# Right-side tiles at multiples of 64 bytes, stores and loads moved to ACT's queue at two stage changes, and a new order of a few products

## The chip, the cores and the metric

The kernel runs on one core of a Trainium2 chip. The metric is the device time of one launch in microseconds (us), smaller is better; a time is given as the median of several runs, and one further execution was taken with the hardware profiler.

The engines are named as the profile names them: PE (matrix products; PEld is its loading of weights), DVE, ACT and POOL (elementwise work), and SP, which only starts DMAs here. Each engine works through its own list of instructions in order; an instruction that waits holds all that stand behind it. SP and ACT can both start DMAs.

## What is computed

One decoder block on x (1024 tokens, width 1024, float32), cut to what matters:

```python
xn   = rms_norm(x, norm1_g)
proj = xn @ w_in                                  # q, k, v | q, f, i, g | two gates
o_sb = stick_breaking_attention(q, k, v)          # 8 heads of 64
o_hg = hgrn2_mixer(q_hg, f_hg, i_hg, g_hg)        # 4 heads of 128, a scan over chunks of 64
y_sb, y_hg = o_sb @ w_branch[:512], o_hg @ w_branch[512:]
mixed = sigmoid(gate_sb) * y_sb + sigmoid(gate_hg) * y_hg
h    = x + mixed @ w_out
hn   = rms_norm(h, norm2_g)
out  = h + (silu(hn @ w_gate) * (hn @ w_up)) @ w_down    # hidden width 2816
```

All of it is float32 to float32 accuracy.

## The kernel before

A float32 product is made of three products of halves: `split` (L229 to L239) rounds an operand to a high part (ACT's CAST) and takes the rest as a low part (DVE's subtraction), and PE multiplies high by high, high by low and low by high. The names in the profile end in h and l for the two parts; a group `f<-fh,oh` has its output first, then the moving operand (128x512, the tokens' side) and then the weights. Every large product is 128 partitions by 512 columns.

The stages, in order:

- Stage 1, to about 702 us: the projection, attention and the scan, laid out by a planner of its own (all on L182). The change leaves its order as it is but for one memset on POOL.
- The merge, about 702 to 791.5 us: `oo`, the outputs of the two branches (`oh0` to `oh7`, `ol0` to `ol7`), moves against `w_branch`: 384 products.
- The wo stage, 791.5 to 878.6 us: `mx` (`ah`, `al`) moves against `w_out`: 384 products in 16 groups, one per row block k and half h of the tokens. Behind each group DVE adds x (`xx`, loaded on SP at L856), SP stores the sum to `h_d` in DRAM (L860), ACT squares it and POOL adds the square to `rr` (L870), the sum for the second norm. DVE and ACT then make the operands `fop` (`fh`, `fl`, L846) of the next stage from it, among them the differences `t5`, `t6`, `t7`.
- The gate and up products, 878.6 to 1317.6 us: a fast product after Strassen and Winograd, seven half-size products instead of eight, for gate and for up, for each of NP = 11 slices p of the hidden width (`winograd`, L963; `prod`, L909; every matmul is on L916): 11 x 2 x 7 x 4 blocks x 3 = 1848 matmuls, with `fop` moving. For the first of all, `begin` is `channel_sums`: it turns `rr` into the norm's factor with four matmuls (L929). At the end of each p, SP stores the activations to `act_d`: one tile `c` of 1 MB (L1008) and four tiles `bs` of 256 KB (L1017).
- The down stage, 1317.6 to 1535.6 us: seven products o in the order `DOWN` (1, 2, 6, 7, 4, 5, 3), each of 11 steps p with four banks d and three matmuls: 132 matmuls for each o. For a step SP loads `ra` (from `wd` or `wd_d`) and `rb` (from `act_d`), 256 KB each; ACT and DVE split both. After o = 1, ACT copies the four banks to `acc1` while the banks go on with o = 2. The residual `h_d` is loaded to `hb` in 16 pieces of 256 KB (L1069), all on SP behind o = 1's last loads, and DVE adds banks and `acc1` to it (L1076, L1077) ahead of the stores to `outT` (L1079).

From the merge on the order within an engine is a scheduler's, made from the order of the code and from the buffers that each instruction needs.

Memory: pools on the left side grow upwards, those with `side="right"` downwards from the top. On the right lie `oo`, `fop` and its sources, some constants and masks of stage 1, and `khl`, `qhh`, `qlz` (attention's keys and queries); on the left `xn`, `mx`, all weights' halves, and `ah`, `al`, `bh`, `bl` of the down stage. In the built kernel the tiles on the right start at 32 bytes beyond a multiple of 64 in each partition, those of the left that move against weights at a multiple of 64.

Of the kernel before, what the change touches and what calls it, by code (L numbers as in the profile page):

```python
# [19 lines left out]
P = 128  # L20
# [182 lines left out]
def hybrid_block(ctx: ExitStack, tc, xT, wi, wb, wo, wg, wu, wd, vec, outT):  # L203
# [40 lines left out]

    rst = ExitStack()
# [585 lines left out]
    with tc.tile_pool(name="wot", bufs=4, reuse_waits="tile") as ot_:  # L831
        seq = [0, 4, 1, 5, 2, 6, 3, 7]
        wq = [get_w(wo[seq.pop(0)])]
        for i in range(4):
# [14 lines left out]
            for e in range(2):  # L849
# [4 lines left out]
                for h in range(2):  # L854
# [5 lines left out]
                    nc.sync.dma_start(h_d[k][:, hs(h)], xx)  # L860
# [4 lines left out]
                    if i == 0 and e == 0:  # L865
                        nc.scalar.activation(rr[h], xx, AF.Square)
                    else:
                        sq = tmp("sq")
                        nc.scalar.activation(sq, xx, AF.Square)
                        nc.gpsimd.tensor_tensor(rr[h], rr[h], sq, op=ALU.add)  # L870
# [65 lines left out]
    with ExitStack() as sta:  # L936
# [24 lines left out]
        def winograd(a, c, begin=None):  # L961

            x, y, z = fb(), fb(), fb()  # L963
            p1 = fa.tile([P, HALF], F32, tag="p1", name="p1")
            if begin:
                for ks in ((0, 1, 2), (3,)):
                    for o, bank in ((1, x), (5, z), (6, y)):
                        prod(bank, a[o], fop[o], True, ks)
                begin()
                nc.scalar.copy(p1, x)  # L970
                nc.vector.tensor_tensor(c[:, 1], y, p1, op=ALU.add)
            else:
                prod(x, a[1], fop[1], True)
                nc.scalar.copy(p1, x)
                prod(y, a[6], fop[6], True)
                nc.vector.tensor_tensor(c[:, 1], y, p1, op=ALU.add)
                prod(z, a[5], fop[5], True)
            prod(y, a[7], fop[7], False)
            prod(x, a[2], fop[2], False)
            nc.vector.tensor_tensor(c[:, 3], y, p1, op=ALU.add)  # L980
            nc.vector.tensor_tensor(c[:, 3], z, c[:, 3], op=ALU.add)
            prod(y, a[4], fop[4], False)
            nc.vector.tensor_tensor(c[:, 2], y, p1, op=ALU.add)
            prod(z, a[3], fop[3], False)
            nc.vector.tensor_tensor(c[:, 1], z, c[:, 1], op=ALU.add)
            return x

        ag = left(wpool, wg, 0)
        for p in range(NP):
# [18 lines left out]
            nc.sync.dma_start(act_d[p][:, :4 * HALF], c.rearrange("p b t -> p (b t)"))  # L1008
# [7 lines left out]
            for b, t in ((4, n7), (5, n6), (6, n5), (7, n4)):  # L1016
                nc.sync.dma_start(act_d[p][:, b * HALF:(b + 1) * HALF], t)  # L1017
# [15 lines left out]
          5: [(d + 4, 1) for d in range(4)], 3: [(d, 1) for d in range(4)]}  # L1033
    bank = [None] * 4
    for o in DOWN:
        first = o in (1, 6, 5)
        for p in range(NP):
            early = o == 1 and p < 4
            wp, tags = bp, btags = dB, ("ah", "al")
            btags = ("bh", "bl")  # L1040
            if early:

                rp = wpool if p < 2 else preB
                raw = rp.tile([P, 1024], F32, tag="w", bufs=2, name="w32")
                ra, rb = raw[:, :512], raw[:, 512:]
                if p < 3:
                    wp = bp = rp
                    tags = btags = ("oh", "ol") if p < 2 else ("ds", "ds")
            else:
                ra = dB.tile([P, HALF], F32, tag="ra", name="ra")  # L1050
                rb = dB.tile([P, HALF], F32, tag="rb", name="rb")
            nc.sync.dma_start(ra, LEFT[o](p))
            nc.sync.dma_start(rb, blk(act_d[p], RIGHT[o]))
            hi, lo = split(ra, wp, tags)
            bh, bl = split(rb, bp, btags)
            for d in range(4):
                if first and p == 0:
                    bank[d] = fb()
                ws = slice(d * P, (d + 1) * P)
                nc.tensor.matmul(bank[d], hi[:, ws], bh, start=first and p == 0, stop=False,  # L1060
                                 skip_group_check=True)
                nc.tensor.matmul(bank[d], hi[:, ws], bl, start=False, stop=False,  # L1062
                                 skip_group_check=True)
                nc.tensor.matmul(bank[d], lo[:, ws], bh, start=False, stop=p == NP - 1,  # L1064
                                 skip_group_check=True)
        if o == 1:
            for k, h in ([(d, 0) for d in range(4)] + [(d, 1) for d in range(8)]
                         + [(d, 0) for d in range(4, 8)]):
                nc.sync.dma_start(hb[k][:, hs(h)], h_d[k][:, hs(h)])  # L1069
            for d in range(4):  # L1070
                nc.scalar.copy(acc1[d], bank[d])
            continue
        for d, (k, h) in enumerate(TO[o]):
            t = hb[k][:, hs(h)]
            if o in (6, 7, 4):
                nc.vector.tensor_tensor(t, t, acc1[d], op=ALU.add)  # L1076
            nc.vector.tensor_tensor(t, bank[d], t, op=ALU.add)  # L1077
            if o in (2, 4, 5, 3):
                nc.sync.dma_start(outT[k][:, hs(h)], t)  # L1079
# [48 lines left out]
```

## Time and profile before

| | us |
|---|---|
| median of 3 runs (1540.65 to 1542.45) | 1542.43 |
| the profiled execution | 1541.46 |
| its span | 1539.7 |
| PE busy | 1515.8 (98%) |
| DVE busy | 1184.3 (77%) |
| ACT busy | 800.4 (52%) |
| POOL busy | 178.8 (12%) |

The profile times one execution. The 1.8 us between its time and its span lie around the program. Busy time counts an engine as busy while an instruction runs; matmuls overlap in PE's pipeline, so what one costs is read from the distance between the starts of two. A bracket behind a row, as in [1.08 <-ACT fh L845], gives the idle time of the engine ahead of it and the instruction whose end ended that. [...]

### The profile page before, as it was taken

Reading aid. Unit: us, or ns where it says so; the run is one execution under the profiler, and the core shown is the slowest. Engines: PE = TensorE matmul, PEld = TensorE weight load, DVE = VectorE, ACT = ScalarE, POOL = GpSimd, SP = SyncE. Lnnn points to the kernel's source line nnn. Section 1 sums busy time; section 2 is a strip of 40 time slices with the busy share of each in tenths; the row PEclk is TensorE's granted clock in tenths of the full one; section 3 lists DMA queues with packets and bytes.
Section 4 is the critical chain, followed back from the end, with each engine's and each line's share of the span. In section 5 each row is a group of like instructions: output and inputs, shape, how many; then the busy total and the mean of one; then the engine's idle time right before and its main releaser. Section 6 shows DMA issues by size and latency. Waiting matters only on the chain.

```text
span 1539.7 us, 20478 instructions
## 1 busy us (share of the span) xinstructions
PE 1515.8 (98%) x7213; PEld 1242.1 (81%) x7213; DVE 1184.3 (77%) x2046; ACT 800.4 (52%) x1503; POOL 178.8 (12%) x202
## 2 busy tenths in 40 slices
PE   8999999999999999999999989999999999999999
PEld 6788888888888888888888868778778888778887
DVE  8899679988898768965567798888877777475553
ACT  7866778678768778454333352233333333254442
POOL 4211111111111101114412200000000000000000
PEclk9999999999999999999999999999999999999999
DMA  5111211111111121245334455666633332787672
GB/s 178 41 43 44 76 33 42 59 39 52 50 52 41 59 69 48 71 160 201 125 107 133 139 163 205 217 211 208 213 136 110 105 105 94 270 274 220 193 220 92
DMA packets 78407, 188.53 MB, mean 122 GB/s; under 512 B 9056, under 2 KB 11104, under 8 KB 76896
## 3 DMA queue, kind: packets, MB, share of 16 engines
q1 hardware_dynamic: 73696, 178.83, 35.5%
q10 hardware_dynamic: 4608, 8.39, 1.5%
q8 instruction: 57, 0.93, 0.3%
q14 instruction: 46, 0.38, 0.1%
HBM read 131.61 MB, written 55.57 MB: 122 GB/s over the span
## 4 chain that ended last, share of the span: by engine, by line
PE 73%; DVE 11%; DMA 6%; ACT 4%; issue 4%; POOL 1%; SPq 1%; DVEq 0%; POOLq 0%; ACTq 0%
PE f L916 25%; PE pj L182 23%; PE ms L182 8%; PE f L1062 4%; PE f L1064 4%; PE f L1060 4%; PE z L182 2%; DMA xx<-xT 2%; DVE ol L238 1%; ACT aa L182 1%; DMA rb<-act_d 1%; POOL s L805 1%; DMA s<-sig_d 1%; DVE aa L182 1%; DVE tail L182 1%
## 5 line engine op out<-in xcount | busy, mean ns | idle before, releaser
L182 PE MATMUL pj<-ah,oh 128*128 128x512 f32 x704 | 286.7, 407 | 2.0 <-POOL oh L182 2.0
L182 PE MATMUL pj<-ah,ol 128*128 128x512 f32 x704 | 277.3, 394 | 0.9 <-DVE ol L182 0.9
L182 PE MATMUL pj<-al,oh 128*128 128x512 f32 x704 | 276.0, 392 | 0.0
L916 PE MATMUL f<-fh,oh 128*128 128x512 f32 x616 | 244.0, 396 | 3.4 <-ACT p L970 1.7
L916 PE MATMUL f<-fl,oh 128*128 128x512 f32 x616 | 243.4, 395 | 0.7 <-DVE fl L846 0.7
L916 PE MATMUL f<-fh,ol 128*128 128x512 f32 x616 | 243.2, 395 | 0.6 <-DVE ol L238 0.6
L237 ACT CAST oh<-w 128x512 fp32r<-128x512 f32 x168 | 102.1, 620 | 175.2 <-PE f L916 137.9
L182 PEld LDWEIGHTS pj<-ah,ol 128*128 128x128 f32 x704 | 132.6, 188 | 31.6 <-DVE ol L182 2.1
L182 PEld LDWEIGHTS pj<-ah,oh 128*128 128x128 f32 x704 | 133.1, 189 | 25.3 <-POOL oh L182 2.9
L182 PEld LDWEIGHTS pj<-al,oh 128*128 128x128 f32 x704 | 133.2, 189 | 22.9 <-issue 0.5
L916 PEld LDWEIGHTS f<-fh,oh 128*128 128x128 f32 x616 | 115.4, 187 | 34.3 <-ACT p L970 2.1
L916 PEld LDWEIGHTS f<-fh,ol 128*128 128x128 f32 x616 | 115.4, 187 | 29.1 <-DVE ol L238 1.0
L916 PEld LDWEIGHTS f<-fl,oh 128*128 128x128 f32 x616 | 115.5, 187 | 29.0 <-DVE fl L846 1.0
L238 DVE TENSOR_TENSOR ol<-w,oh 128x512 fp32r<-128x512 f32 x168 | 114.7, 690 | 30.0 <-ACT oh L237 29.8
L1062 PE MATMUL f<-bl,ah 128*128 128x512 f32 x296 | 117.0, 395 | 1.3 <-DVE bl L238 1.3
L1060 PE MATMUL f<-bh,ah 128*128 128x512 f32 x296 | 114.6, 391 | 3.7 <-ACT bh L237 3.7
L182 DVE TENSOR_TENSOR_SCAN aa<-aa,ww 128x128 f32<-128x128 f32 (+3 forms) x96 | 92.3, 975 | 33.4 <-ACT aa L182 23.8
L182 POOL TENSOR_SCALAR oh<-w 128x512 fp32r<-128x512 f32 x84 | 70.9, 844 | 394.0 <-PE pj L182 348.6
L1064 PE MATMUL f<-bh,al 128*128 128x512 f32 x296 | 116.6, 394 | 0.0
L238 DVE TENSOR_TENSOR al<-ra,ah 128x512 fp32r<-128x512 f32 x73 | 50.4, 690 | 72.0 <-ACT ah L237 71.9
L237 ACT CAST ah<-ra 128x512 fp32r<-128x512 f32 x73 | 45.5, 623 | 101.8 <-PE f L1062 93.7
L182 ACT ACTIVATE aa<-aa 128x512 f32<-128x512 f32 (+3 forms) x128 | 69.1, 552 | 4.9 <-DVE aa L182 4.0
(273 smaller groups left out, 2996.7 us busy)
## 6 DMA issues: line engine op xcount, KB each, us to landing
w<-wi SPq DMA_DIRECT2D x42, 512.0 KB, 3.6
rb<-act_d SPq DMA_DIRECT2D x73, 256.0 KB, 4.1
w<-wg SPq DMA_DIRECT2D x22, 512.0 KB, 3.9
w<-wu SPq DMA_DIRECT2D x22, 512.0 KB, 4.1
w<-wd SPq DMA_DIRECT2D x22, 512.0 KB, 6.8
wd_d<-ds SPq DMA_DIRECT2D x44, 256.0 KB, 5.4
act_d<-c SPq DMA_DIRECT2D x11, 1024.0 KB, 3.9
act_d<-bs SPq DMA_DIRECT2D x44, 256.0 KB, 3.5
```

The costliest lines, as they stand in the source:

```text
L182: fn(*[a.real() if isinstance(a, View) else a for a in args], **{k: v.real() if isinstance(v, View) else v for k, v in kw.items()})
L237: pin(nc.scalar.copy(hi, src))
L238: pin(nc.vector.tensor_tensor(lo, src, hi.bitcast(F32), op=ALU.subtract))
L805: nc.gpsimd.tensor_tensor(s[:, hs(h)], s[:, hs(h)], rr1[h], op=ALU.mult)
L916: nc.tensor.matmul(out, a[i][:, ws], bl[k][j], start=start and k == 0 and i + j == 0, stop=k == 3 and i == 1, skip_group_check=True)
L1060: nc.tensor.matmul(bank[d], hi[:, ws], bh, start=first and p == 0, stop=False, skip_group_check=True)
L1062: nc.tensor.matmul(bank[d], hi[:, ws], bl, start=False, stop=False, skip_group_check=True)
L1064: nc.tensor.matmul(bank[d], lo[:, ws], bh, start=False, stop=p == NP - 1, skip_group_check=True)
```

## The change

1. A tile `edge` of 32 bytes per partition is put at the top of the right side, so that all tiles of the right side lie 32 bytes lower, at multiples of 64. POOL sets it to zero once.
2. In the wo stage, the 16 stores to `h_d` go from SP's queue to ACT's.
3. There, the 14 adds to `rr` go from POOL to DVE.
4. In the first gate product (p = 0) the order is new. Before: products 1, 5, 6 over the blocks 0 to 2, then block 3 of each, then `begin`, then ACT's copy of bank x to `p1`. Now: product 1 whole, the copy, product 5 whole, product 6 over blocks 0 to 2, product 2 (into bank x), block 3 of product 6, then `begin`. Product 2 stood behind product 7 before.
5. The five stores to `act_d` of the last p go to ACT's queue.
6. The 16 loads of `hb` go to ACT's queue, two in each of the steps p = 3 to 10 of o = 1.
7. In the last of the down products (o = 3) the last three steps run bank by bank: bank 0 takes its nine matmuls, then its add and its store follow, then bank 1. The loop body is cut into `operands`, `step` and `finish` for that.

The diff, with the parts that only regroup the down loop left out:

```diff
+    edge = ctx.enter_context(tc.tile_pool(name="edge", bufs=1, side="right"))
+    nc.gpsimd.memset(edge.tile([P, 8], F32, name="edge"), 0.0)
     rst = ExitStack()
...
-                    nc.sync.dma_start(h_d[k][:, hs(h)], xx)
+                    nc.scalar.dma_start(h_d[k][:, hs(h)], xx)
...
-                        nc.gpsimd.tensor_tensor(rr[h], rr[h], sq, op=ALU.add)
+                        nc.vector.tensor_tensor(rr[h], rr[h], sq, op=ALU.add)
...
             if begin:
-                for ks in ((0, 1, 2), (3,)):
-                    for o, bank in ((1, x), (5, z), (6, y)):
-                        prod(bank, a[o], fop[o], True, ks)
+                prod(x, a[1], fop[1], True)
+                nc.scalar.copy(p1, x)
+                prod(z, a[5], fop[5], True)
+                prod(y, a[6], fop[6], True, range(3))
+                prod(x, a[2], fop[2], False)
+                prod(y, a[6], fop[6], True, (3,))
                 begin()
-                nc.scalar.copy(p1, x)
                 nc.vector.tensor_tensor(c[:, 1], y, p1, op=ALU.add)
...
             prod(y, a[7], fop[7], False)
-            prod(x, a[2], fop[2], False)
+            if not begin:
+                prod(x, a[2], fop[2], False)
...
-            nc.sync.dma_start(act_d[p][:, :4 * HALF], c.rearrange("p b t -> p (b t)"))
+            store = nc.scalar.dma_start if p == NP - 1 else nc.sync.dma_start
+            store(act_d[p][:, :4 * HALF], c.rearrange("p b t -> p (b t)"))
...
-                nc.sync.dma_start(act_d[p][:, b * HALF:(b + 1) * HALF], t)
+                store(act_d[p][:, b * HALF:(b + 1) * HALF], t)
...
+    HB = ([(d, 0) for d in range(4)] + [(d, 1) for d in range(8)] + [(d, 0) for d in range(4, 8)])
+    LAST = 3
...
+        final = o == DOWN[-1]
+        for p in range(NP - LAST if final else NP):
+            ops = operands(o, p)
+            if o == 1 and p >= 3:
+                for k, h in HB[2 * p - 6:2 * p - 4]:
+                    nc.scalar.dma_start(hb[k][:, hs(h)], h_d[k][:, hs(h)])
             for d in range(4):
                 if first and p == 0:
                     bank[d] = fb()
...
+                step(d, p, ops, first and p == 0)
         if o == 1:
-            for k, h in ([(d, 0) for d in range(4)] + [(d, 1) for d in range(8)]
-                         + [(d, 0) for d in range(4, 8)]):
-                nc.sync.dma_start(hb[k][:, hs(h)], h_d[k][:, hs(h)])
             for d in range(4):
                 nc.scalar.copy(acc1[d], bank[d])
...
+        elif not final:
+            for d in range(4):
+                finish(o, d)
+    rest = [(p, operands(o, p)) for p in range(NP - LAST, NP)]
+    for d in range(4):
+        for p, ops in rest:
+            step(d, p, ops, False)
+        finish(o, d)
```

Where the order on an engine becomes another, at the three places that the prediction speaks of.

DVE, from the wo stage's end into the first gate products, before: the last two blocks are under way (`xx` for the last one stands ahead of these rows), `parts` are the pieces of `rr` for `channel_sums`, `fl` the low parts of `fop`, `ol` those of weights.

```order
L238 TENSOR_TENSOR ol<-w_9157,oh 128x512
L862 TENSOR_SCALAR yy<-xx,vt 128x512
L925 TENSOR_TENSOR parts<-rr_8379,parts 128x512
L881 TENSOR_TENSOR t_9120<-yy 128x512
L882 TENSOR_TENSOR yy<-t_9120,yy 128x512
L925 TENSOR_TENSOR parts<-rr_8380,parts 128x512
L238 TENSOR_TENSOR ol<-w_9193,oh 128x512
L846 TENSOR_TENSOR fl<-yy,fh 128x512
L846 TENSOR_TENSOR fl<-t_9120,fh 128x512
```

The same place now:

```order
L928 TENSOR_TENSOR parts<-rr_8384,parts 128x512
L862 TENSOR_TENSOR xx<-pj,xx 128x512
L865 TENSOR_SCALAR yy<-xx,vt 128x512
L884 TENSOR_TENSOR t_9125<-yy 128x512
L873 TENSOR_TENSOR rr_8385<-rr_8385,sq 128x512
L885 TENSOR_TENSOR yy<-t_9125,yy 128x512
L238 TENSOR_TENSOR ol<-w_9198,oh 128x512
L902 TENSOR_TENSOR w_9200<-w_9198,w_9200 128x512
L849 TENSOR_TENSOR fl<-yy,fh 128x512
L903 TENSOR_TENSOR s_9206<-w_9200 128x512
L849 TENSOR_TENSOR fl<-t_9125,fh 128x512
```

The adds to `rr` are among DVE's work, the second `parts` has moved behind the operands, and two operations for weights (`w`, `s`) stand between them.

SP at the change from the gate and up products to the down stage, before: loads for o = 1, step 0 and 1 (`w_12594`, `w_12621`), two pieces of `hb`, the last stores, then step p = 4's loads.

```order
L1052 DMA w_12594<-wd 128x512
L1053 DMA w_12594<-act_d_118 128x512
L1052 DMA w_12621<-wd 128x512
L1053 DMA w_12621<-act_d_119 128x512
L1069 DMA hb_12582<-h_d_140 128x512
L1069 DMA hb_12583<-h_d_141 128x512
L1008 DMA act_d_128<-c 128x2048
L1017 DMA act_d_128<-bs 128x512 x4
L1052 DMA ra<-wd 128x512
L1053 DMA rb<-act_d_122 128x512
```

The same place now (the stores are those of the last p but one):

```order
L1015 DMA act_d_132<-c 128x2048
L1024 DMA act_d_132<-bs 128x512 x4
L1060 DMA w_12599<-wd 128x512
L1061 DMA w_12599<-act_d_123 128x512
L1060 DMA w_12626<-wd 128x512
L1061 DMA w_12626<-act_d_124 128x512
L1060 DMA ra<-wd 128x512
L1061 DMA rb<-act_d_127 128x512
```

And ACT there now, where before these rows held only the casts:

```order
L1087 DMA hb_12587<-h_d_145 128x512
L1087 DMA hb_12588<-h_d_146 128x512
L1015 DMA act_d_133<-c 128x2048
L1024 DMA act_d_133<-bs 128x512 x4
L237 CAST ah<-w_12672 128x512
L237 CAST bh<-w_12672 128x512
L1087 DMA hb_12589<-h_d_147 128x512
L237 CAST ah<-ra 128x512
L237 CAST bh<-rb 128x512
L1087 DMA hb_12590<-h_d_148 128x512
```

SP's queue has no `hb` and no last stores left; ACT's has them ahead of and between its splits (`w_12672` is the raw tile of step p = 3).

ACT where o = 1 ends and o = 2 begins, before:

```order
L237 CAST ah<-ra 128x512
L237 CAST bh<-rb 128x512
L1071 COPY acc_12590<-f 128x512
L1071 COPY acc_12591<-f 128x512
L1071 COPY acc_12592<-f 128x512
L1071 COPY acc_12593<-f 128x512
```

and now, where the first two rows belong to o = 2's first step:

```order
L237 CAST ah<-ra 128x512
L237 CAST bh<-rb 128x512
L237 CAST ah<-ra 128x512
L1094 COPY acc_12595<-f 128x512
L237 CAST bh<-rb 128x512
L1094 COPY acc_12596<-f 128x512
L1094 COPY acc_12597<-f 128x512
L1094 COPY acc_12598<-f 128x512
```

Before, the two casts ahead of the copies are those of o = 1's last step; now three casts of o = 2 come ahead of the first copy.

## Rows read from the trace of the kernel before

**Rows 1.** The page's first part, PE: busy us, share of the span, instructions.

```profile
PE 1515.8 (98%) x7213; PEld 1242.1 (81%) x7213; DVE 1184.3 (77%) x2046; ACT 800.4 (52%) x1503; POOL 178.8 (12%) x202
```

**Rows 2.** The timeline of PE's matmuls in four stretches, the first and the last row of each: the merge (66 matmuls in all), the wo stage (68), the gate and up products (66) and the down stage (68). Columns: start and length in us, engine, line, operation, output and inputs.

```profile
747.67 0.39 PE L303 MATMUL pj<-ol,oh 128*128 128x512 f32 x1
...
762.84 0.40 PE L302 MATMUL z<-oh,oh 128*128 128x512 f32 x1
...
799.74 0.39 PE L302 MATMUL pj<-ah,oh 128*128 128x512 f32 x1
...
814.92 0.39 PE L303 MATMUL pj<-al,oh 128*128 128x512 f32 x1
...
1198.80 0.39 PE L916 MATMUL f<-fl,oh 128*128 128x512 f32 x1
...
1213.96 0.40 PE L916 MATMUL f<-fh,oh 128*128 128x512 f32 x1
...
1439.72 0.39 PE L1064 MATMUL f<-bh,al 128*128 128x512 f32 x1
...
1454.91 0.39 PE L1060 MATMUL f<-bh,ah 128*128 128x512 f32 x1
```

**Rows 3.** The timeline of PE's matmuls where the gate products start: the first product, and all that PE waited for in the first 17 us.

```profile
878.62 0.40 PE L916 MATMUL f<-fh,oh 128*128 128x512 f32 x1
...
881.91 0.50 PE L916 MATMUL f<-fh,ol 128*128 128x512 f32 x1 [0.56 <-DVE ol L238]
...
888.38 0.49 PE L916 MATMUL f<-fh,oh 128*128 128x512 f32 x1 [1.08 <-ACT fh L845]
889.53 0.50 PE L916 MATMUL f<-fl,oh 128*128 128x512 f32 x1 [0.66 <-DVE fl L846]
...
892.91 0.50 PE L916 MATMUL f<-fh,oh 128*128 128x512 f32 x1 [1.71 <-ACT p L970]
...
895.55 0.50 PE L916 MATMUL f<-fh,oh 128*128 128x512 f32 x1 [0.51 <-DVE g L971]
```

**Rows 4.** The timelines of DVE, POOL and SP at the same place, one after the other (SPq is SP's queue; the length is that of the issue).

```profile
882.94 0.69 DVE L859 TENSOR_TENSOR xx<-pj,xx 128x512 f32<-128x512 f32 x1 [1.09 <-DMA xx<-xT]
...
884.54 1.80 DVE L925 TENSOR_TENSOR parts<-rr,parts 128x512 fp32r<-128x512 f32 x1
...
889.39 0.69 DVE L846 TENSOR_TENSOR fl<-t,fh 128x512 fp32r<-128x512 f32 x1
...
884.50 1.29 POOL L870 TENSOR_TENSOR rr<-rr,sq 128x512 f32<-128x512 f32 x1 [3.81 <-ACT sq L869]
...
879.05 0.38 SPq L856 DMA_DIRECT2D xx<-xT  x1
```

**Rows 5.** Busy time of the engines in one stretch of the gate and up products: from and to, us, then busy us and instructions of PE, PEld, DVE, ACT and POOL, the granted clock, the DMA engines' share and GB/s.

```profile
900.00:1310.00 410.00, 409.85 (x1755) 328.15 (x1754) 340.07 (x546) 130.64 (x217) 0.00 (x0) 1.00 0.47 160
```

**Rows 6.** The timeline of PE's matmuls around its two holes in the down stage.

```profile
1328.24 0.39 PE L1064 MATMUL f<-bh,al 128*128 128x512 f32 x1
1330.58 1.50 PE L1060 MATMUL f<-bh,ah 128*128 128x512 f32 x4 [1.95 <-ACT bh L237]
1331.88 0.63 PE L1062 MATMUL f<-bl,ah 128*128 128x512 f32 x1
...
1334.81 0.39 PE L1064 MATMUL f<-bh,al 128*128 128x512 f32 x1
...
1351.15 0.39 PE L1064 MATMUL f<-bh,al 128*128 128x512 f32 x1
1353.25 1.19 PE L1060 MATMUL f<-bh,ah 128*128 128x512 f32 x4 [1.71 <-ACT bh L237]
1355.72 0.80 PE L1062 MATMUL f<-bl,ah 128*128 128x512 f32 x1 [1.28 <-DVE bl L238]
...
1358.76 0.39 PE L1064 MATMUL f<-bh,al 128*128 128x512 f32 x1
```

**Rows 7.** Busy time by stretches there, columns as in rows 5; the granted clock is the third figure from the end.

```profile
1331.00:1334.00 3.00, 3.00 (x9) 2.31 (x8) 2.96 (x6) 2.79 (x6) 0.00 (x0) 0.55 1.05 398
...
1335.00:1352.00 17.00, 16.54 (x73) 13.33 (x71) 6.20 (x11) 5.54 (x10) 0.00 (x0) 1.00 1.05 386
```

**Rows 8.** The timeline of SP's queue from the end of the up products on. A row with a count covers that many issues, from the first to the end of the last.

```profile
1307.26 5.92 SPq L1069 DMA_DIRECT2D hb<-h_d  x2
1319.21 0.32 SPq L1008 DMA_DIRECT2D act_d<-c  x1
...
1323.47 0.61 SPq L1052 DMA_DIRECT2D ra<-wd  x1
...
1333.27 9.11 SPq L1069 DMA_DIRECT2D hb<-h_d  x14
```

**Rows 9.** The timelines of ACT and of DVE where o = 2 starts.

```profile
1349.53 2.62 ACT L1071 COPY acc<-f 128x512 f32<-128x512 f32 x4 [10.83 <-PE f L1064]
...
1350.15 4.30 DVE L1076 TENSOR_TENSOR hb<-hb,acc 128x512 f32<-128x512 f32 x7 [10.72 <-ACT acc L1071]
```

**Rows 10.** The end: the timelines of DVE and of PE (its last matmul), and the DMA issues of the last 7 us (KB of each, median us from issue to landing).

```profile
1533.99 2.73 DVE L1077 TENSOR_TENSOR hb<-f,hb 128x512 f32<-128x512 f32 x4 [12.55 <-PE f L1064]
...
1535.60 0.39 PE L1064 MATMUL f<-bh,al 128*128 128x512 f32 x1
...
outT<-hb SPq DMA_DIRECT2D x4, 256.0 KB, 2.1
```

More of the change, by code (lines that the diff above doesn't have):

```diff
@@ L1033, in hybrid_block, with operands @@
           5: [(d + 4, 1) for d in range(4)], 3: [(d, 1) for d in range(4)]}
+    HB = ([(d, 0) for d in range(4)] + [(d, 1) for d in range(8)] + [(d, 0) for d in range(4, 8)])
+    LAST = 3
     bank = [None] * 4
+    def operands(o, p):
+        wp = bp = dB
+        tags, btags = ("ah", "al"), ("bh", "bl")
+        if o == 1 and p < 4:
+            rp = wpool if p < 2 else preB
+            raw = rp.tile([P, 1024], F32, tag="w", bufs=2, name="w32")
+            ra, rb = raw[:, :512], raw[:, 512:]
+            if p < 3:
+                wp = bp = rp
+                tags = btags = ("oh", "ol") if p < 2 else ("ds", "ds")
+        else:
+            ra = dB.tile([P, HALF], F32, tag="ra", name="ra")
+            rb = dB.tile([P, HALF], F32, tag="rb", name="rb")
+        nc.sync.dma_start(ra, LEFT[o](p))
+        nc.sync.dma_start(rb, blk(act_d[p], RIGHT[o]))
+        return split(ra, wp, tags) + split(rb, bp, btags)
@@ new lines, in step, with finish @@
+    def step(d, p, ops, start):
+        hi, lo, bh, bl = ops
+        ws = slice(d * P, (d + 1) * P)
+        for i, (l, r) in enumerate(((hi, bh), (hi, bl), (lo, bh))):
+            nc.tensor.matmul(bank[d], l[:, ws], r, start=start and i == 0,
+                             stop=p == NP - 1 and i == 2, skip_group_check=True)
+    def finish(o, d):
+        k, h = TO[o][d]
+        t = hb[k][:, hs(h)]
+        if o in (6, 7, 4):
+            nc.vector.tensor_tensor(t, t, acc1[d], op=ALU.add)
+        nc.vector.tensor_tensor(t, bank[d], t, op=ALU.add)
+        if o in (2, 4, 5, 3):
+            nc.sync.dma_start(outT[k][:, hs(h)], t)
@@ L1035, in hybrid_block @@
     for o in DOWN:
         first = o in (1, 6, 5)
[L1037 to L1055, printed above, removed]
+        final = o == DOWN[-1]
@@ L1058, in hybrid_block @@
                     bank[d] = fb()
[L1059 to L1065, printed above, removed]
+                step(d, p, ops, first and p == 0)
         if o == 1:
-            for k, h in ([(d, 0) for d in range(4)] + [(d, 1) for d in range(8)]
-                         + [(d, 0) for d in range(4, 8)]):
-                nc.sync.dma_start(hb[k][:, hs(h)], h_d[k][:, hs(h)])
             for d in range(4):
                 nc.scalar.copy(acc1[d], bank[d])
[L1072 to L1079, printed above, removed]
+        elif not final:
[6 more added lines that the diff above has]
+        finish(o, d)
 def _layout(inputs):
```

## The prediction

> **What bounds the kernel now.** I began with the busy table of the page. PE is busy for 98% of the span [rows 1], so a change can only pay in two ways: by shortening the time of a matmul, or by closing one of PE's few holes. I then read the timeline of PE in the four dense stages, for the step from one matmul's start to the next; one 128x512 matmul is shown as 0.39 to 0.40 us long in all of them, but they overlap, so only the step is the price. In the merge stage 65 steps take 762.84 - 747.67 = 15.17 us, 233.4 ns each; in the wo stage 67 steps take 15.18 us, 226.6 ns; in the gate and up products 65 steps take 15.16 us, 233.2 ns; in the down stage 67 steps take 15.19 us, 226.7 ns [rows 2]. Type, shape and order (three products of split halves) are alike, and no stretch has a hole. What differs is the moving operand: oh/ol of the merge and fh/fl of the gate products lie on the right side of the memory, at addresses 32 beyond a multiple of 64; ah/al of wo and bh/bl of the down stage lie on the left at multiples of 64. Stage 1's xn is on the left too.
>
> The holes come next: the timeline of PE where the gate products start [rows 3] and where the down stage starts [rows 6], and then what stood in the way on DVE, POOL and SP [rows 4, 8] and on ACT and DVE [rows 9]. Last, the tail [rows 10].
>
> **The change part by part.**
>
> *The edge tile.* It costs one POOL memset in the start-up, where PE waits for loads and splits; I price it at nothing, and at its own length, below a microsecond, if it is not covered. It moves every tile of the right side down by 32 bytes. If the residue of the address sets the step, the gate and up products, 11 x 2 x 7 x 12 = 1848 matmuls, save 233.2 - 226.6 = 6.6 ns each, 12.2 us, and the merge stage's 384 save 6.8 ns each, 2.6 us. [...] The lower bound is zero: no tile of the right side with the other residue is timed cleanly in this trace, so "right side" and "32 beyond" can't be told apart. In stage 1, khl moves in 192 score products and ident in 384 transposes; at 6.7 ns that is at most 3.9 us, but there much of PE's time is set by waits, so I take 0.5 (0 to 3.9). DVE stays under PE: in the gate and up products it is busy for 340 of 410 us [rows 5], 83%, or 85% of the shortened time.
>
> [...]
>
> *The start of the gate products.* From the first product at 878.62 to the one at 895.55 there are 48 (36, four channel sums and 8): 16.93 - 48 x 0.2332 = 5.7 us lost, in five holes [rows 3]. The causes are in [rows 4]. SP queues the store of xx ahead of the load of the last xx: the store waits for DVE's xx, so the load goes at 879.05 only and DVE's add starts 1.09 us late, at 882.94. The POOL add of rr (1.29 us) stretches what DVE runs beside it: 1.80 us at 884.54 instead of 0.68. So the last operand, fl from t, starts at 889.39, 6.45 us after that add. With the stores on ACT, the loads run ahead, and the add can follow the last wo product, some 0.7 us after 878.62. The same 6.45 us later, less about 1.1 us of stretching, makes 884.7 + 0.7. The new order asks for it after x, z, three parts of y and x += a2, 45 matmuls or 10.2 us: 888.8. That is 3 us of cover, so the holes before 888.38 and 889.53 go, and so does the one at 881.91, where DVE's split waited on a stretched operation. The one at 892.91 (1.71 us for ACT's copy of p) goes because the copy now follows x by two products. The one at 895.55 (0.51 us, DVE's g) can stay: y + p1 still stands between y's last part and y += a7, with only four sums (0.9 us) to cover it and other work ahead of it on DVE. I take 5.0 of 5.7; bounds 3.5 (two holes stay) and 5.7. The 14 adds of rr cost DVE 14 x 0.69 = 9.7 us of the wo stage, and spare it about 14 x 0.7 to 1.1 us of stretching; at nothing. The 16 stores cost ACT an issue each, with ACT about half idle there; behind each wait stands ACT's Square of the same xx, which needs the same DVE add, so nobody waits longer.
>
> *The start of the down stage.* From 1328.24 to 1334.81 there are 12 steps: 6.57 - 12 x 0.2267 = 3.9 us lost; from 1351.15 to 1358.76 again 12: 7.61 - 2.72 = 4.9 us. Together 8.8 [rows 6]. Only 1.95 us of the first and 1.71 + 1.28 of the second are waits. [...]
> The first hole waits for p = 4's bh. SP went to that load at 1323.47 only, since h loads waiting for PE (1307.26) and the five stores of the last activations (from 1319.21) stood ahead [rows 8]. In the new order on SP p = 4's loads follow what the FFN's end frees, 1317.56: 5.9 us earlier against a wait of 1.95. Behind the waits that now stand on ACT (two h loads, c, bs) are the splits of p = 3 and 4: the last bs is ready on DVE at about 1323 in any case, p = 3 is asked for 8.2 us after 1317.56, at 1325.7, and ACT takes 0.65 us for a tile of this size (2.62 for four, [rows 9]). That is 1 to 2 us of cover.
> The second hole: 14 h loads in 9.11 us from 1333.27 stand on SP ahead of all loads for o = 2 [rows 8], then ACT's four copies of acc (1349.53) and DVE's seven adds of acc (4.30 us from 1350.15) ahead of its splits [rows 9]. In the new order the loads for o = 2 follow p = 10's directly, p = 0's two splits stand ahead of the copies, and the adds come later. What decides is then the DMA: c and bs (2.1 MB), seven steps of 0.52 MB, 14 h loads of 0.26 MB and the first of o = 2 make 10.2 MB; at the 386 GB/s of [rows 7] that is 26.5 us, for 132 matmuls or 29.9 us. It fits with 3 us to spare, but the copies stand behind the split of p = 1's ra, and PE's first product on bank 0 waits for the first copy. I take 7.8 of 8.8, keeping one short wait; bounds 4 (one hole comes back whole) and 8.8.
> [...]
>
> *The last steps bank by bank.* The last matmul starts at 1535.60, the last of DVE's four adds ends at 1533.99 + 2.73 = 1536.72, the last store is issued then and lands about 2.1 us later, the median of the four [rows 10], after which 0.9 us of closing events are left of the span. A wait of one store for another would show in that median, so the three ahead hardly delay it. After the change there is still one add and one store behind the last matmul. So I price this part at 0, bounds 0 and 0.7 (one add). The operands of p = 8 to 10 are asked for up to 24 matmuls (5.4 us) sooner, but DVE had been idle for 12.55 us at that point [rows 10], so they are there.
>
> **Sum.** 12.2 + 2.6 + 0.5 + 5.0 + 7.8 + 0 = 28.1 us. The profiled execution took 1541.46 us (span 1539.7), so 1513.4; the median of three runs is 1.0 above the profiled one, so 1514. Own range: gains from 12.2 + 2.6 + 3.5 + 4 = 22.3 (1520) to 14.8 + 3.9 + 5.7 + 8.8 + 0.7 = 33.9 (1508, and 1507 against the profiled time).
>
> **Rivals.**
> *The residue does nothing* (the right side itself, or the tile's kind, sets the step). Only the edges pay: 5.0 + 7.8 = 12.8, 1529.6. For it: the confusion named above. [...] 0.13.
> *The down stage's holes come back*, for ACT's in-order queue or for the DMA: 20.3 gained, 1522. For it: only 1 to 3 us of cover in both places. Against: loads run up to 5.9 us sooner. 0.14.
> *Slower: ACT is held in every step of o = 1.* [...] 0.03.
> *The change doesn't do what it says*: no term is realised, within 3 us of before. 0.03.
>
> **Chances.** Forecast 0.67, its range 1507 to 1520; with the returning holes 0.81, so the range is 1507 to 1523. A measurement can tell 0.2% (3.1 us) from no change. Faster 0.94, same 0.03, slower 0.03.
>
> **What the profile would show.** Right: steps of 226 to 227 ns in the merge and in the gate and up products, which then last 1848 x 0.2267 = 419 us plus at most one short hole; no PE wait over 1 us in the first 17 us of the gate products; a granted clock of 1.00 at the down stage's start; the tail unchanged, 4.1 us from the last matmul's start to the end of the span. Wrong: steps still at 233 ns, which takes away half of the sum; or a PE wait for ACT's bh or acc in the down stage with the clock at half behind it.

## The result

| | us |
|---|---|
| before, median of 4 runs | 1541.54 |
| after, median of 4 runs (1528.22 to 1531.17) | 1529.57 |
| ratio, 95% interval | 0.9923 [0.9906, 0.9940] |
| the profiled execution after | 1531.17 |
| its span | 1529.4 |

The kernel is 0.77% faster, by 12 us, where 28 were forecast: it lies 6.6 us above the upper end of the range. The time is that of the first rival to a tenth of a microsecond (1529.6, "the residue does nothing"), and yet that rival is wrong, as the first rows after show. The two profiled executions differ by 1541.46 - 1531.17 = 10.3 us.

The steps of PE. The timeline of PE's matmuls after, first and last row of 68 each, in the merge and in the gate products:

```profile
747.62 0.39 PE L305 MATMUL pj<-oh,oh 128*128 128x512 f32 x1
...
762.80 0.39 PE L306 MATMUL pj<-ol,oh 128*128 128x512 f32 x1
...
1198.76 0.39 PE L919 MATMUL f<-fh,ol 128*128 128x512 f32 x1
...
1213.95 0.39 PE L919 MATMUL f<-fh,oh 128*128 128x512 f32 x1
```

67 steps take 15.18 and 15.19 us, 226.6 and 226.7 ns; before it was 233.4 and 233.2 [rows 2]. That gain came in whole. By stages, from the starts of the first product of each:

| stage | before | after | gained | forecast |
|---|---|---|---|---|
| start to the first gate product | 878.62 | 877.86 | 0.8 | 3.1 |
| gate and up products | 438.94 | 435.37 | 3.6 | 17.2 |
| down stage, to its last matmul | 218.04 | 212.06 | 6.0 | 7.8 |
| the rest of the span | 4.1 | 4.1 | 0 | 0 |

The loss is in the gate and up products. 1848 products of 0.2332 us and four sums are 431.9 us, so 7.1 were lost in holes before; at 0.2267 they are 419.9, so 15.5 are lost after. What PE waited for there after (line, us in all, times, longest; `p` is ACT's copy `p1`, `g` and `c` are the tiles in which DVE adds up the gate and the up products):

```profile
PE f L919 <- ACT p L970: 7.1, 1, 7.1
PE f L919 <- DVE g L981: 3.0, 5, 0.8
PE f L919 <- DVE g L986: 1.0, 1, 1.0
```

The first is new in size and place. The timeline of PE's matmuls at the start of the gate products after:

```profile
877.86 0.39 PE L919 MATMUL f<-fh,oh 128*128 128x512 f32 x1
...
885.12 0.39 PE L919 MATMUL f<-fh,ol 128*128 128x512 f32 x1
892.64 0.79 PE L919 MATMUL f<-fh,oh 128*128 128x512 f32 x1 [7.14 <-ACT p L970]
893.24 0.63 PE L919 MATMUL f<-fl,oh 128*128 128x512 f32 x1
...
897.08 0.42 PE L919 MATMUL f<-fl,oh 128*128 128x512 f32 x1
```

PE runs 33 products without a hole, where before there was one [rows 3], stops for 7.1 us, and then steps by 0.43 us for the next ten (893.24 to 897.08 is 9 steps): 9.5 us lost, and 1.3 more at 905.3, at its wait for `g` on L986. What held it, on DVE, ACT and SP:

```profile
881.33 0.69 DVE L862 TENSOR_TENSOR xx<-pj,xx 128x512 f32<-128x512 f32 x1
...
885.43 0.69 DVE L884 TENSOR_TENSOR t<-yy 128x512 f32<-128x512 f32 x1 [2.89 <-DMA h_d<-xx]
...
877.82 0.33 ACTq L863 DMA_DIRECT2D h_d<-xx  x1
...
886.76 0.62 ACT L927 CAST parts<-rr 128x512 fp32r<-128x512 f32 x1 [3.20 <-DVE rr L873]
...
892.01 0.58 ACT L970 COPY p<-f 128x512 f32<-128x512 f32 x1
...
875.34 0.80 SPq L230 DMA_DIRECT2D w<-wu  x2
876.19 0.42 SPq L948 DMA_DIRECT2D w<-wd  x1
876.66 0.44 SPq L949 DMA_DIRECT2D w<-wd  x1
```

This reads backwards. PE's next product is product 2, which adds to bank x; bank x is read by ACT's copy to `p`; the copy starts at 892.01 only, behind the casts of the last operand on ACT. They, and `parts` at 886.76, wait for DVE. DVE had idled for 2.89 us at 885.43 until the landing of a store to `h_d`: `t`, the tile t7, takes the buffer of an older `xx`, the one stored at 877.82. SP, no longer held by the stores, had by then started four loads of weights of 512 KB each (875.34 to 876.66), and the store lay behind them in the DMA engines. From 877.9 to 881.5 packets moved for SP's queue (q1) alone, 1.22 MB of them, and none for ACT's (q10), on which the store stands. The queue's packets, MB and share of the 16 engines' time in that stretch, and the store's KB and us from issue to landing:

```profile
q1 hardware_dynamic: 345, 1.22, 99.5%
h_d<-xx ACTq DMA_DIRECT2D x1, 256.0 KB, 7.5
```

Its landing took 7.5 us; issue to landing of the 16 stores, minimum, median and maximum:

```profile
DMA to landing us min/median/max: 2.0/3.5/7.5
```

Before, the maximum was 4.2 us, and nobody waited for one.

The down stage. Its holes of 1.95, 1.71 and 1.28 us [rows 6] have become these, on the timeline of PE after (and one of 0.31 us at 1341.68):

```profile
1338.31 0.50 PE L1068 MATMUL f<-bl,ah 128*128 128x512 f32 x1 [0.19 <-DVE bl L238]
...
1345.54 0.50 PE L1068 MATMUL f<-bh,ah 128*128 128x512 f32 x1 [1.07 <-ACT acc L1094]
```

and the clock holds (busy time by stretches, columns as in rows 5; the first row is the start of the gate products, with the granted clock, PE's as a share of its full one, at 0.50 behind the hole of 7.1 us):

```profile
893.00:896.00 3.00, 3.00 (x8) 2.32 (x8) 3.00 (x6) 0.82 (x2) 0.00 (x0) 0.50 0.53 139
1313.30:1330.00 16.70, 16.70 (x75) 13.82 (x74) 9.59 (x15) 5.57 (x10) 0.00 (x0) 1.00 0.87 310
1330.00:1344.00 14.00, 13.50 (x58) 10.43 (x57) 4.74 (x9) 4.13 (x9) 0.00 (x0) 1.00 1.05 386
```

The end: the last matmul.

```profile
1525.29 0.39 PE L1068 MATMUL f<-bh,al 128*128 128x512 f32 x1
```

From the last matmul's start to the end of the span it is 1529.4 - 1525.29 = 4.1 us, as before [rows 10].

### The profile page after: what moved, and what is told of

It reads as the page before. It is cut to its first block, busy times and chain, and to the rows that moved or that the text cites. A ratio compares the mean times of both kernels' runs of the same rounds, so it can differ in the third digit from the quotient of the medians.

```text
span 1529.4 us, 20448 instructions
## 1 busy us (share of the span) xinstructions
PE 1500.8 (98%) x7213; PEld 1241.2 (81%) x7213; DVE 1179.9 (77%) x2060; ACT 799.1 (52%) x1503; POOL 160.5 (10%) x189
## 4 chain that ended last, share of the span: by engine, by line
PE 72%; DVE 12%; DMA 6%; ACT 4%; issue 4%; POOL 2%; SPq 0%; POOLq 0%; ACTq 0%; DVEq 0%
PE pj L182 24%; PE f L919 20%; PE f L1068 12%; PE ms L182 8%; PE z L182 2%; DMA w<-wu 2%; PE pj L306 2%; PE pj L305 2%; PE pj L307 2%; DVE ol L238 2%; DMA s<-sig_d 1%; ACT aa L182 1%; DMA rb<-act_d 1%; POOL s L808 1%; DMA h_d<-xx 1%
```

## The experiments

Each was timed next to the kernel before on the same chip, so the ratio is the figure to compare. 0.001 is 1.54 us. Two ratios whose intervals overlap are not told apart by the times; what is said of them beyond that is read from one profiled execution of each.

| kernel | median us | ratio to before, 95% interval |
|---|---|---|
| after | 1529.57 | 0.9923 [0.9906, 0.9940] |
| edge tile alone | 1533.25 | 0.9938 [0.9923, 0.9953] |
| all but the edge tile | 1538.60 | 0.9982 [0.9973, 0.9990] |
| 32 bytes ahead of xn (one run) | 1542.32 | |
| 32 bytes ahead of the weights | 1531.10 | 0.9937 [0.9921, 0.9952] |
| first gate product in the old order | 1528.96 | 0.9918 [0.9905, 0.9931] |
| products 7 and 2 swapped | 1541.03 | 1.0008 [0.9997, 1.0018] |
| swapped, and t7 elsewhere | 1542.33 | 1.0017 [1.0007, 1.0027] |
| product 2 in a bank of its own, t7 elsewhere | 1526.87 | 0.9915 [0.9902, 0.9929] |
| edge tile and down stage | 1525.45 | 0.9904 [0.9889, 0.9919] |
| that, four subtractions left out | 1525.55 | 0.9906 [0.9893, 0.9919] |
| rr on POOL | 1526.25 | 0.9913 [0.9897, 0.9929] |
| h stores on SP | 1522.26 | 0.9880 [0.9865, 0.9894] |
| h stores on SP, old order | 1524.70 | 0.9895 [0.9876, 0.9914] |
| t7 elsewhere | 1527.66 | 0.9919 [0.9903, 0.9936] |

### What sets the step of a matmul

**The edge tile alone** (before, with part 1 of the change).

> The kernel before with the 32-byte edge tile alone. Theory (residue of the address): the merge and the gate and up products step at 226.7 ns, 14.8 us saved; but where DVE only just kept up with the slower products it now falls behind, so 3 to 5 us come back as PE's waits for DVE in the merge's last group and in the slices p = 2 to 6: about 1531 (1529 to 1533). Rival (those waits come from the new order and queues, not from the faster products): no new waits, 1527.

Measured 0.9938, 9.6 us of the 14.8 that the steps give. PE's longest waits in the gate and up products:

```profile
PE f L918 <- DVE g L978: 5.5, 5, 1.7
```

The five waits for DVE's g are those of the changed kernel, and longer. They belong to the faster products, not to the new order; the theory holds for these slices. For the merge it isn't shown: there this execution lost 0.4 us.

**All but the edge tile.**

```diff
-    edge = ctx.enter_context(tc.tile_pool(name="edge", bufs=1, side="right"))
-    nc.gpsimd.memset(edge.tile([P, 8], F32, name="edge"), 0.0)
```

> The changed kernel without the edge tile: all but the shift. Theory (ACT's copy of p holds PE by the order on ACT, whatever the speed of a matmul): PE still waits about 7 us for ACT's copy of p in the first gate product and the clock falls behind it, some 4 to 5 us more lost there than before; the down stage gains about 6.5: 1539 to 1541. Rival (the wait is there because the products are faster): no wait over 2 us at that place, 1531 to 1533.

Measured 0.9982. PE waits for the copy of p here too, at products that step by 233.4 ns (29 steps from 879.76 to 886.53):

```profile
892.74 0.79 PE L917 MATMUL f<-fh,oh 128*128 128x512 f32 x1 [5.81 <-ACT p L968]
```

Of the stages, the gate and up products are 3.3 us longer than before (442.26 against 438.94) and the down stage 6.3 shorter (211.75). So the wait is the new order's and the queues' doing, and not that of the faster products. The two parts add up: 0.0062 + 0.0018 = 0.0080, against 0.0077 for both.

**32 bytes ahead of xn, on the left.**

```diff
+    pad = ctx.enter_context(tc.tile_pool(name="pad", bufs=1))
+    nc.gpsimd.memset(pad.tile([P, 8], F32, name="pad"), 0.0)
     xst = ExitStack()
     xn = a_set(xst.enter_context(tc.tile_pool(name="xnp", bufs=1)))
```

> The kernel before with 32 bytes put ahead of xn on the left side, so that xn, mx and the down stage's operands lie 32 beyond a multiple of 64 as well; nothing on the right moves. Theory (the residue sets the step): 512-column products in the wo stage and the down stage step at 233 ns, and so do most in stage 1: 2.6 + 6.2 + up to 14 us longer, about 1560 (1550 to 1565). Rival (the right side itself sets the step): 226.7 ns there as before, 1541.

Measured 1542.32, a miss by 18 us. The time is near the rival's, but not for its reason: the first gate product starts 6.3 us later than before (884.90), while the gate and up products take 1.9 us less (437.01) and the down stage 3.5 less (214.54). Its timeline of PE, first and last row of each stretch: the wo stage (66 rows), a gate product (45), an up product (55) and the down stage (68):

```profile
799.74 0.39 PE L303 MATMUL pj<-al,oh 128*128 128x512 f32 x1
...
814.90 0.40 PE L302 MATMUL pj<-ah,oh 128*128 128x512 f32 x1
...
929.63 0.39 PE L918 MATMUL f<-fl,oh 128*128 128x512 f32 x1
...
939.90 0.39 PE L918 MATMUL f<-fh,oh 128*128 128x512 f32 x1
...
949.65 0.39 PE L918 MATMUL f<-fh,oh 128*128 128x512 f32 x1
...
961.89 0.39 PE L918 MATMUL f<-fh,oh 128*128 128x512 f32 x1
...
1439.67 0.39 PE L1064 MATMUL f<-bl,ah 128*128 128x512 f32 x1
...
1454.85 0.39 PE L1066 MATMUL f<-bh,al 128*128 128x512 f32 x1
```

The steps are 15.16 / 65 = 233.2 ns, 10.27 / 44 = 233.4, 12.24 / 54 = 226.7 and 15.18 / 67 = 226.6. All four have their moving operand 32 beyond a multiple of 64. The up product and the down stage are fast all the same, and they are the two whose weights were moved by the 32 bytes as well (the up weights' pool and the down stage's lie above the pad, the gate's and wo's weights below it). So my theory, that the residue of the moving operand alone sets the step, falls. The new one: a step is short, 226.6 to 226.7 ns, where weights and moving operand start at the same residue of 64 bytes, and long, 233.2 to 233.4 ns, where they differ. Of the cases that differ the runs have one only, weights at 0 and the moving operand at 32, and why the residues matter no run shows.

**32 bytes ahead of the weights, on the left**, so that everything lies 32 beyond.

```diff
+    pad = ctx.enter_context(tc.tile_pool(name="pad", bufs=1))
+    nc.gpsimd.memset(pad.tile([P, 8], F32, name="pad"), 0.0)
     wpool = ctx.enter_context(tc.tile_pool(name="wpool", bufs=4))
```

> The kernel before with the 32 bytes put ahead of the weights' pool on the left, so that weights and moving operands of every stage lie 32 beyond a multiple of 64; no large operand of a product is left at a multiple of 64. Theory (the step is short where weights and moving operand have the same residue, whatever it is): 226.7 ns in all stages, as with the edge tile, 1531 to 1534. [...]

Measured 0.9937, the same as with the edge tile (0.9938). Its gate and up products, first and last of 68 rows:

```profile
1198.76 0.39 PE L918 MATMUL f<-fl,oh 128*128 128x512 f32 x1
...
1213.95 0.39 PE L918 MATMUL f<-fh,ol 128*128 128x512 f32 x1
```

That is 15.19 / 67 = 226.7 ns. No large operand lies at a multiple of 64, and the step is the short one: in these runs equality counts (226.6 ns with both at 0 in the wo stage before, 226.7 with both at 32 here), not the boundary.

### What holds PE at the start of the gate products

**The first gate product in its old order**, all else as changed (part 4 undone).

> The changed kernel with the first gate product in its order of before; all else is kept. Theory (product 2 in bank x made PE wait for ACT's copy of p): that wait goes, but the last operand is still late, as DVE's t7 waits for the landing of an h store, so PE waits 4 to 5 us at block 3 of the first products: 1525 to 1528. Rival (the stores on ACT's queue are the only cause): the same loss under another name, 1529 to 1531.

Measured 0.9918, as the changed kernel: the rival's case in time. PE's wait has moved, to the sums' operands and to the last operand:

```profile
PE f L932 <- DVE parts L928: 3.2, 1, 3.2
...
PE f L919 <- ACT fh L848: 1.5, 1, 1.5
```

In this execution the gate and up products take 432.70 us against 435.37 in the changed kernel, but the merge, whose code is the same, 90.61 against 88.77. So what the new order costs with the stores on ACT stays open between nothing and some 3 us.

**Product 2 in a bank of its own**, the sums last, and t7 in the buffer of an earlier square.

```diff
-                prod(x, a[2], fop[2], False)
+                x2 = fb()
+                prod(x2, a[2], fop[2], True)
                 prod(y, a[6], fop[6], True, (3,))
-                begin()
...
+            if begin:
+                begin()
+                nc.vector.tensor_tensor(p1, x2, p1, op=ALU.add)
+                return p1
...
-                        t7, t6 = tmp("t7"), blk[0, 0]
+                        t7, t6 = sqs[1, 0] if i == 3 else tmp("t7"), blk[0, 0]
```

> The changed kernel with the dependence on ACT's copy of p taken away in the first gate product: product 2 gets a bank of its own and is added by DVE at the end, channel_sums comes last, and t7 takes the buffer of an earlier square instead of that of the last xx, whose store has to land first. Theory (DVE's queue from the last xx to the add of y and p is the bound there, about 14.5 us of work, 2.9 of idling): PE waits next for DVE's add, until about 893, and only the 2.9 us of idling are gained, 1525 to 1528. Rival (ACT's place for the copy of p is the bound): no wait over 2 us there, 1519 to 1522.

Measured 0.9915. The copy of p no longer matters, and PE waits for the next late thing:

```profile
PE f L919 <- DVE g L981: 3.8, 4, 1.9
PE f L919 <- ACT oh L237: 2.8, 1, 2.8
PE f L919 <- DVE ol L238: 1.1, 1, 1.1
PE f L919 <- DVE g L976: 1.0, 1, 1.0
```

2.8 us for a cast of weights, 1.1 for DVE's low part, 1.0 for DVE's add of y and p (PE goes on at 896.96). The time is the theory's, though the waits are spread over ACT and DVE and the add is not the next of them. With the copy out of the way the gain is about 1 us by the ratios, and inside their intervals. The profiled execution is the longest of the six (1530.01 us), so its waits may be longer than usual.

**The adds of rr on POOL again** (part 3 undone).

> The changed kernel with the adds of rr on POOL again. Theory (DVE's queue between the last xx and the add of y and p is the bound at the start of the gate products, and the adds are part of it): PE's wait for ACT's copy of p is 1 to 3 us shorter, 1526 to 1528. Rival (POOL's adds stretch DVE's operations by as much as they spare): within 1 us of the changed kernel.

Measured 0.9913: between the two, 1.5 us of gain by the ratios, inside the intervals. Inconclusive. One of its six executions took 5328 us; the ratio is that of the other five, and their median is 1525.90. In the profiled one, at 1531.90 the longest of these, the waits of the start are short again (at most 1.6 us each), but 6.2 us went to g.

**The h stores on SP again** (part 2 undone).

> The changed kernel with the 16 h stores on SP's queue again. Theory (the stores' place matters little, as DVE's t7 waits for the landing of the last one in either queue): within 1.5 us of the changed kernel, 1528 to 1531. Rival (ACT holds its casts for the stores): 3 us or more faster.

Measured 0.9880, 6.6 us better than the changed kernel, with intervals that don't overlap, and the best of all: the theory falls, and the rival's size came. Timelines of PE (all its waits in that stretch) and DVE, and the engines' busy time behind PE's wait (columns as in rows 5):

```profile
886.76 0.50 PE L919 MATMUL f<-fh,oh 128*128 128x512 f32 x1 [1.83 <-ACT p L970]
891.65 0.50 PE L919 MATMUL f<-fh,oh 128*128 128x512 f32 x1 [0.70 <-DVE g L976]
...
878.82 0.69 DVE L862 TENSOR_TENSOR xx<-pj,xx 128x512 f32<-128x512 f32 x1
...
880.07 0.69 DVE L884 TENSOR_TENSOR t<-yy 128x512 f32<-128x512 f32 x1
...
886.00:890.00 4.00, 3.24 (x14) 2.70 (x15) 4.00 (x8) 1.88 (x4) 0.00 (x0) 1.00 0.48 141
```

DVE takes the last xx at 878.82, not 881.33 (the first gate product starts at 876.38, not 877.86, so 1.0 us of that is DVE's own), and t follows at 880.07 without idling; PE waits 1.83 us for the copy and not 7.14, and the granted clock stays at 1.00. The gate and up products take 428.62 us against 435.37. The 1.5 us ahead of them are the merge's, whose code is the same. Issue to landing of the stores:

```profile
DMA to landing us min/median/max: 2.0/2.3/4.2
```

On SP the last two stores are issued at 874.88 and 879.54, ahead of the loads of weights at 875.77 and at 879.91 and 880.39, and none of the 16 took more than 4.2 us to land, against 7.5 on ACT's queue. The stores' place mattered, and the rows show one way, by the time to landing. That what ACT held back had no share isn't shown: from 791 to 897 us DVE waited 5.5 us for ACT's casts of weights in the changed kernel and 2.7 here.

**t7 in the buffer of an earlier square**, the stores still on ACT (the last edit of the diff above, alone).

> The changed kernel with t7 in the buffer of an earlier square, so that nothing waits for the landing of an h store; the stores stay on ACT. Theory (an h store on ACT is queued in the DMA engines behind four weight loads of 512 KB that SP now starts early, and DVE's t7 waits 2.9 us for its landing): DVE idles no more there, PE's wait for the copy of p falls from 7.1 to about 4.3 us, 1525 to 1527. The rest of the 7 us that the stores on SP's queue gave would then be that DVE reaches the last xx later. Rival (the landing is no cause, only ACT's casts behind the issues): PE's wait stays near 7, 1529.

Measured 0.9919. DVE idles no more at t, PE's wait falls to 5.1 us, but the landing has a new victim. ACT's timeline:

```profile
876.54 0.33 ACTq L863 DMA_DIRECT2D h_d<-xx  x1
...
883.16 0.63 ACT L872 ACTIVATE sq<-xx 128x512 f32<-128x512 f32 x1 [3.96 <-DMA h_d<-xx]
```

With one tile fewer in the pool, it is now the square `sq` that takes the stored `xx`'s buffer, and ACT waits 3.96 us for the landing. So by the rows the landing is a cause, and moving one tile away from it shortens PE's wait by 2.0 us, less than the 2.9; in the time (0.9919 against 0.9923) the two kernels aren't told apart.

**The h stores on SP, the first gate product in its old order.**

> The changed kernel with the h stores on SP and the first gate product in its order of before; the adds of rr stay on DVE. Theory (with the stores out of the way the new order pays, as predicted at first): 1 to 3 us slower than the kernel with the stores on SP and the new order, 1523 to 1525. Rival (the new order is worth nothing, the gain of that kernel over the one with edge tile and down stage alone is all from the adds): as that kernel, 1522.

Measured 0.9895 against 0.9880. The direction is the theory's, 2.3 us, but the intervals overlap: what the new order is worth with the stores on SP isn't settled by these runs.

**Edge tile and down stage only** (parts 2, 3 and 4 undone).

> The changed kernel with the wo stage and the first gate product as before: the edge tile, the queue moves at the down stage and the last steps bank by bank are kept. Theory (the h stores on ACT, the adds of rr on DVE and the new order together cost time): the edge tile alone took 1533, the down stage gives 6.3 more, so 1526 to 1527. Rival (those three are neutral): as the changed kernel, 1529 to 1530.

Measured 0.9904, the theory's case: by the ratios those three parts together cost 2.9 us, though the intervals just overlap. In the profiled executions the gate and up products take 429.89 us here and 435.37 in the changed kernel.

### What holds PE at the starts of p = 2 to 6

**Products 7 and 2 swapped** in every gate and up product.

```diff
                 prod(z, a[5], fop[5], True)
-            prod(y, a[7], fop[7], False)
-            if not begin:
                 prod(x, a[2], fop[2], False)
+            prod(y, a[7], fop[7], False)
```

> The changed kernel with products 7 and 2 swapped in every gate and up product, so that PE has 24 matmuls (5.4 us) and not 12 between product 6 and product 7, which waits for DVE's add of y and p. Theory (the waits at the starts of p = 2 to 6 are DVE's in-order queue, behind by under 1 us): they go, 3 to 4.4 us less than the changed kernel, 1525 to 1527. Rival (DVE is behind by more, and the next product waits for it): under 1 us less, 1529.

Measured 1.0008: 13 us slower than the changed kernel, a miss. The waits for g (L981) are gone, as meant, but there are others:

```profile
PE f L919 <- DVE c L985: 7.8, 5, 2.1
PE f L919 <- ACT p L970: 5.9, 1, 5.9
```

Product 2 had covered DVE's two adds between products 7 and 4 (c, L985 here); taken from there, PE waits for those, in the up products of p = 0 to 4, up to 2.1 us each; the mean granted clock of this execution is 0.993, against 0.996 in the changed kernel. One product can't cover both places.

**The same with t7 in the buffer of an earlier square.**

> The changed kernel with t7 in the buffer of an earlier square, and products 7 and 2 swapped as in the kernel with the swap alone. Theory: PE's wait for ACT's copy of p is shorter by about 2.9 us, the idling of DVE for the landing of the h store, and by the clock's share, and the waits of p = 2 to 6 go: 1521 to 1524. Rival (the landing is not what holds the chain): as the kernel with the swap alone.

Measured 1.0017, a miss for the same cause (8.3 us for c); PE's wait for the copy of p was 4.9 us.

**DVE's four subtractions of down_sums left out**, on the kernel with edge tile and down stage alone; ACT copies raw quarters instead.

```diff
-            sub(s7, a11, a21)
-            sub(s6, a22, s7)
-            nc.vector.tensor_tensor(s5, s6, a11, op=ALU.add)
-            sub(s3, a12, s6)
+            for s, r in ((s7, a11), (s6, a21), (s5, a22), (s3, a12)):
+                nc.scalar.copy(s, r)
```

> The kernel with edge tile and down stage alone, with DVE's four subtractions of down_sums in each slice p left out: ACT copies the raw quarters of w_down in their place, so five of the seven down products take wrong weights. It spares DVE 4 x 0.6 us in each of 11 slices and changes no product. Theory (PE's waits for g at the starts of p = 2 to 6 are DVE's queue running behind the faster products): they go, 3 to 5 us less than the kernel with edge tile and down stage alone. Rival (they hang on something else, a load or ACT): they stay, within 1 us.

The five waits for g, which the kernel it was made from shows as

```profile
PE f L919 <- DVE g L979: 3.9, 5, 1.1
```

have become

```profile
PE f L919 <- DVE c L977: 1.3, 1, 1.3
...
PE f L919 <- DVE g L977: 0.7, 1, 0.7
```

one wait for g and one for c, 2.0 us instead of 3.9. So they are DVE's queue. But the time is the same (0.9906 against 0.9904): in time this is the rival's case. In the profiled execution the gate and up products are 1.2 us shorter (428.73 against 429.89), and the down stage is 2.8 us longer (215.05 against 212.26), with a wait of 1.46 us at 1340.5 that the other hasn't. Whether the edit brings that wait isn't settled; one execution of each differs by as much.

## Why the prediction was wrong, step by step

**The step of a matmul** (12.2 + 2.6): right in size, wrong in its reason. All 14.8 us are in the steps of the profile. The reason, the residue of the moving operand alone, fell with the pad ahead of xn, where two stretches with that operand at 32 step by 226.7 and 226.6 ns. The rival "the residue does nothing" is refuted, although its time was met: 32 bytes took the step from 233.2 to 226.7 ns.

**"DVE stays under PE"**, 83% to 85% busy: right as an average and wrong as a cover. In the merge DVE's t came 1.4 us late once (787.9 us), and the merge gained 0.8 us (88.77 against 89.60) where 2.6 were forecast; in the gate and up products the later slices lose 4.7 us in holes (15.5 less 10.8 at the start), against 1.4 before. I had no term for either. The edge tile alone shows the later slices' waits. The merge's loss is no fixed cost: with the same code, it took from 87.04 us (stores on SP) to 90.61 (first gate product in the old order) in the profiled executions with the short step.

**The start of the gate products** (5.0, bounds 3.5 and 5.7): the step that failed. It lost 10.8 us where 5.7 were lost before. Three things in it were wrong. "With the stores on ACT, the loads run ahead": they did, and it is these loads behind which the store then lay; I had looked at who waits for the issue, not for the landing. The store took 7.5 us to land, and in the first 3.7 us of that only the loads' packets moved. "The add can follow the last wo product, some 0.7 us after": DVE had its own arrears and took it at 881.33, 3.3 us after that product's end. "The copy now follows x by two products": in the code, not on ACT, where it stands behind the casts of the last operand; and the new order asks for it at the 34th product, since product 2 adds to the bank that it reads. The bound had no case in which the loss grows. Whether the adds of rr cost nothing, as priced, isn't settled: with them on POOL the ratio is 0.9913, against 0.9923.

**The start of the down stage** (7.8): 6.0, within its bounds. The long holes went, and with them the lower clock: before, it was 0.50 from 1331.88 to 1334.43, with steps of 0.42 us, and from 1355.72 to 1358.44; now it is 1.00 from 1313.3 to 1350. Which of parts 5 and 6 did it, no run tells apart. The copies of acc did come late, as the text feared, by 1.07 us. The DMA engines were full, with a share of 1.05 at 386 GB/s from 1330 to 1344.

**The last steps** (0): right; the tail is 4.1 us in both.

**Stage 1** (0.5): not seen; the first 878 us gained 0.8 in all, and the merge has all of it.

The terms as they came: 14.8 for the steps, -5.1 at the start of the gate products, -3.3 at the later slices (together 8.4 us of holes more than before), -1.8 in the merge, 6.0 in the down stage: 10.6, against 10.3 of the two executions. The version with the stores on SP beats both kernels: 1522.26 us, 0.9880.

## What to carry to other kernels

When a store goes to another queue to free the loads behind it, ask what those loads do to the landing of the store, and which buffer waits for that landing. When products are reordered for the sake of one late operand, look at every reader of the banks that the new order writes again, and at its place on its own engine's list and not only in the code. And a time that agrees with a rival is no evidence for the rival: only the rows told these two apart.

## What had not been expected of the hardware

- A 128x512 float32r matmul steps by 226.6 to 226.7 ns where weights and moving operand start at the same residue of 64 bytes (both 0 in the changed kernel, both 32 in the two kernels with a pad), and by 233.2 to 233.4 ns where the weights are at 0 and the moving operand at 32 (before, and in the gate products and the wo stage of the pad ahead of xn). The reverse and other residues weren't tried.
- A hole in PE is not always followed by the lower clock. Behind the 7.1 us at 885 the granted clock was 0.50; before the change, a hole of 1.95 us and one of 1.71 + 1.28 us in the down stage had brought it (0.55 from 1331 to 1334 [rows 7], 0.70 from 1354 to 1357), while in the same execution one of 1.71 us at 892.91 [rows 3] did not (1.00 from 885 to 900), nor with the stores on SP one of 1.83 us at 886.76 (1.00 from 886 to 890). So in these runs the price of a hole can't be read from its length alone.
- A store of 256 KB to `h_d` took from 2.0 to 7.5 us to land on ACT's queue in the changed kernel, the longest behind four loads of weights, and from 2.0 to 4.2 on SP's, before and with the stores back there.
